# Modulation weights in tiles of four row blocks instead of two

## The chip, the core and the metric

The kernel runs on one NeuronCore of a Trainium2 chip. TensorE (PE) does matrix products, VectorE (DVE), ScalarE (ACT) and GpSimd (POOL) work on elements, and the queue of SyncE (SP) issues nearly all transfers between HBM and the on-chip memory SBUF. TensorE writes its results to PSUM, from where DVE and ACT fetch them. The metric is the device time of one execution in microseconds.

## The reference, cut to what matters

The program is two layers of a diffusion backbone over 1024 latent and 256 context tokens of width 1024. Each layer normalises the tokens, scales and shifts them, projects them by `w_in`, runs four mixers (gated linear attention GLA, neighbourhood attention NA, a diagonal state space model S5, pooling), gates their outputs, projects by `w_out`, normalises and adds. Scale, shift and gate come from a small product, and this is the part that the change touches:

```python
for l in range(DEPTH):   # 2 layers
    shift, scale, gate = jnp.split(jax.nn.silu(c) @ w_mod[l] + b_mod[l], 3, axis=-1)
    shift_c, scale_c, gate_c = jnp.split(jax.nn.silu(c_ctx) @ w_mod[l] + b_mod[l], 3, axis=-1)
    h = rmsnorm(x, g_pre[l]) * (1.0 + scale[:, None]) + shift[:, None]
    ...
    x = x + gate[:, None] * rmsnorm(y @ w_out[l], g_post[l])
```

`w_mod[l]` is 1024 x 3072 in fp32, 12 MB for a layer, and it meets two vectors only: the product is nearly all weight transfer. Everything is fp32.

## The kernel before, in words

The planner that turns the Python into instruction streams keeps one fixed order for each engine. It takes what is ready by its own estimate of times, by priority, and priority is the place in the program unless `later()` adds an amount. So instructions of one helper can be spread between those of others.

`modulation` (line 187) walks over pieces of 512 columns of `w_mod`: two pieces for each of scale, shift and gate. The 1024 rows of a piece are eight blocks of 128 rows. A tile `wm` holds two blocks ([128, 2, 512], 512 KB, 2 KB runs in HBM); a piece takes four tiles. `products` (line 194) takes two tiles, that is four blocks, and gives each block its own group of 32 TensorE columns: block k goes to `state[0][32k:32k+32]`, with `csil`, the silu of the two vectors, as stationary operand. An fp32 matmul is two instructions in the trace, so a call of `products` is eight MATMUL instructions of 512 columns (four from either tile), and a piece is two calls. `rows` copies the PSUM tile to SBUF (line 203). `mod_finish` (line 222) adds the four column groups by another small product and writes either `mcol` (scale and shift) or, for the gate, rows of `dM` in HBM.

`modulation` is a generator: it yields after each load, and whoever holds it calls `next`. `startup` (line 1476) drains that of layer 0's scale and shift, four pieces, before the first normalisation can finish: sixteen loads, tiles in six buffers. The remaining eight pieces run in `run` (line 1532 on): six while layer 0 projects (gate of layer 0, then scale and shift of layer 1) and two while layer 1 does (gate of layer 1). There `self.mods` is advanced by one step after each result of `proj_tok` (line 338) and `proj_cols` (line 323), with three buffers of `wm` and one PSUM bank `pm`. The parameter `lag` (1) and the list `todo` set how far a product stays behind its loads: the first load of a pair is issued with one product still open, the second only after all open products.

Around it in these stages: `s5_proj` and `na_proj` (lines 318 and 334 are the matmuls of all projections), the GLA chunks (lines 934 to 1062), after them S5 and its filler `proj_gates` (line 318 again, evacuated on lines 346 and 347), and the NA phase (lines 1284 to 1460). A branch that all engines pass (line 1555) stands between S5 and NA.

Of the kernel before, what the change touches and what calls it, by code (L numbers as in the profile page):

```python
# [70 lines left out]
class Kernel:  # L71
# [112 lines left out]
        for i in range(2):  # L184
            v.tensor_copy(self.csil[:, :, 32 * i:32 * i + 2], th.rearrange("p (a b) n -> p a b n", b=2)[:, :, i])

    def modulation(self, l, pieces, raws, psum, pool, lag=1):


        nc = self.nc  # L190
        wm = self.a["w_mod"][l].rearrange("(k p) f -> p k f", p=128)
        todo = []

        def products(state, k0, *ws):
            if k0 == 0:
                state.append(psum())
            for k in range(4):
                nc.tensor.matmul(state[0][32 * k:32 * k + 32, :], lhsT=self.csil[:, (k0 + k) // 2, 2 * (k % 2):2 * (k % 2) + 32], rhs=ws[k // 2][:, k % 2, :],
                                 start=(k0 == 0), stop=(k0 == 4))

        def rows(state):
            state.append(self.t([128, 512], "mrow", 2, pool))
            nc.scalar.copy(state[1], state[0])

        for third, q in pieces:
            c0 = third * 1024 + q * 512
            state = []
            for k0 in (0, 4):
                ws = []
                for k in (k0, k0 + 2):  # L210
                    while sum(f.func is products for f in todo) > (lag if k == k0 else 0):
                        todo.pop(0)()
                    ws.append(self.t([128, 2, 512], *next(raws)))
                    nc.sync.dma_start(ws[-1], wm[:, k:k + 2, c0:c0 + 512])
                    yield
                todo.append(partial(products, state, k0, *ws))
            todo += [partial(rows, state), partial(self.mod_finish, l, third, q, state, psum, pool)]
        for f in todo:
            f()
            yield  # L220
# [1255 lines left out]
    def startup(self):  # L1476

        nc, a = self.nc, self.a
        self.silu_c()
        cyc = itertools.cycle  # L1480
        pm = lambda: self.ps2.tile([128, 512], F32, tag="pm", bufs=2, name=self.nm("pm"))
        mods = self.modulation(0, ((1, 0), (0, 0), (1, 1), (0, 1)), cyc([("wm", 6)]), pm, self.mix)
        self.npb = 4
        groups = []
        left = True
        for gi, (t0, n, steps) in enumerate(ORD):
            if not left:
                for g in groups:
                    self.norm_cols(0, *g)
                groups = []  # L1490
            xs = [self.t([128, 1024], "xt", XTB) for _ in range(n)]
            ss = self.t([128, 4], "nss", 3)
            for i, x in enumerate(xs):
                nc.sync.dma_start(x, a["tok"][(t0 + i) * 128:(t0 + i + 1) * 128, :])
                junk = self.t([128, 1024], "stg", 4, self.stg, dtype=mybir.dt.bfloat16)
                if SQ[t0 + i] == "1":
                    nc.vector.tensor_tensor_reduce(junk, x, x, 1.0, 0.0, ALU.mult, ALU.add, ss[:, i:i + 1])
                else:
                    nc.scalar.activation(junk, x, AF.Square, accum_out=ss[:, i:i + 1])
            rs = self.rsqrt(ss[:, :n], [128, n], 1.0 / D, EPS, f"nr{n}")  # L1500
            for i, x in enumerate(xs):
                nc.vector.tensor_scalar(x, x, rs[:, i:i + 1], None, op0=ALU.mult)
            groups.append((t0, xs))
            if gi == WP and WP:
                W = self.load_w(a["w_in"][0][:, 128:416], 288, engines=(cyc([nc.gpsimd]),cyc([nc.vector]), cyc([nc.gpsimd, nc.vector]), cyc([nc.vector,nc.gpsimd]))[SWE])
            for _ in range(steps):
                next(mods, None)
            if steps == 99:
                left = False
            if gi == WP and not WP:  # L1510
                W = self.load_w(a["w_in"][0][:, 128:416], 288, engines=(cyc([nc.gpsimd]),cyc([nc.vector]), cyc([nc.gpsimd, nc.vector]), cyc([nc.vector,nc.gpsimd]))[SWE])
        for g in groups:
            self.norm_cols(0, *g)
        return W

    def run(self):
        nc, a, tc = self.nc, self.a, self.tc
        self.load_consts()
        self.s5p = [None] * DEPTH
        with self.phase("start", True):  # L1520
            with self.phase("x"):
                W = self.startup()
            self.gla_proj(0, False, W)
            self.s5_params(0)
            self.npb = 6
        for l in range(DEPTH):
            last = l == DEPTH - 1
            if last:
                self.gla_proj(l, last)
                with self.phase("par", True):  # L1530
                    self.s5_params(l)
            with self.phase("mods", True) as pool:
                psum = self.ps2
                pm = lambda: psum.tile([128, 512], F32, tag="pm", bufs=1, name=self.nm("pm"))
                todo = ((1, (2,)),) if last else ((0, (2,)), (1, (1, 0)))
                self.npb = 5
                flag = self.gla(l, last)
                self.npb = 6
                raws = itertools.cycle([("wm", 3, pool)])
                mods = itertools.chain(*(self.modulation(i, [(third, q) for third in th for q in range(2)], raws, pm, pool) for i, th in todo))  # L1540
                self.mods = mods
                self.s5_proj(l)
                with self.later():
                    self.na_proj(l, last)
                    for _ in self.mods:
                        pass
            self.npb = 2
            self.s5(l, last)
            self.npb = 6
            ch = CHUNKS[1:] if last else CHUNKS  # L1550
            with self.later():
                self.pool_proj(l, last)
                for m in range(SPLIT[l]):
                    self.proj_gates(l, m, ch)
            with tc.If(nc.values_load(flag, min_val=0, max_val=1) != 0):
                self.gla_general(l, last)
            with self.later(50000, True) as after:
                for m in range(SPLIT[l], 8):
                    self.proj_gates(l, m, ch if m < 8 - RES[l] else ch[:-1])
            self.na(l, last)  # L1560
            tc.cur_priority = after[0]
            with self.phase("out", True):
                self.npb = 2
                for m in range(8 - RES[l], 8):
                    self.proj_gates(l, m, ch[-1:])
                self.out_tiles(l, last)
                self.npb = 6
# [158 lines left out]
```

## Time and profile before

| what | value |
|---|---|
| three runs | 1386.04, 1388.77, 1389.81 us (median 1388.77) |
| profiled execution, its own time | 1390.5 us |
| span of its instructions | 1388.7 us |
| PE busy | 1265.2 us (91%), 6958 matmul instructions |
| PE weight loads | 1011.0 us (73%) |
| DVE / ACT / POOL busy | 66% / 42% / 15% |
| DMA | 231 MB, mean 166 GB/s |
| mean granted TensorE clock | 0.968 |
| matmuls of the modulation (line 198) | 192 instructions |

The profile is of one execution. Times in it count from the first instruction. A matmul's end is modelled, so neighbours overlap in the listing; the distance from one start to the next is what a matmul takes from the stream. The last 1.8 us of the execution's own time lie around the span.

### The profile page before, as it was taken

What the parts mean: (1) busy time and instruction counts of PE and PEld (TensorE: products, weight loads), DVE (VectorE), ACT (ScalarE), POOL (GpSimd) and SP (SyncE); (2) the same over time, 40 slices, a digit from 0 to 9 for tenths busy, and PEclk for the clock granted to TensorE, in tenths of its full rate; (3) what the DMA queues carried; (4) which work ended last, traced back from release to release, by engine and by line L of the source; (5) the groups of instructions that cost most, each with busy time, mean ns of one, the idle gap of its engine ahead of it and who ended that gap; (6) DMA issues with size and microseconds to landing.
All of it is one profiled execution on the core that took longest, in us unless ns stands there. A gap on an engine that the chain in (4) does not pass through costs nothing. (4 is left out here: it accounts for less than half of the span.)

```text
span 1388.7 us, 20066 instructions
## 1 busy us (share of the span) xinstructions
PE 1265.2 (91%) x6958; PEld 1011.0 (73%) x6958; DVE 912.5 (66%) x2269; ACT 584.9 (42%) x1218; POOL 203.8 (15%) x212
## 2 busy tenths in 40 slices
PE   5799999999999999988989999999899998777897
PEld 2698967667777678767878989768667776665676
DVE  2777577456388548773866787586654884776383
ACT  2653443223333347663555644443323333665321
POOL 0100000001100024351410000000112100234220
PEclk9699999999999999999999999999999999998999
DMA  9436685752533267746832475865215535754662
GB/s 330 157 116 224 192 252 166 217 182 76 164 127 113 81 184 197 209 141 208 246 124 92 124 230 188 246 183 157 79 46 185 166 108 161 201 150 139 192 210 91
DMA packets 223477, 231.07 MB, mean 166 GB/s; under 512 B 47016, under 2 KB 176552, under 8 KB 223040
## 3 DMA queue, kind: packets, MB, share of 16 engines
q1 hardware_dynamic: 221776, 227.14, 53.8%
q10 hardware_dynamic: 1584, 2.49, 0.5%
q8 instruction: 58, 0.95, 0.3%
q14 instruction: 59, 0.48, 0.1%
HBM read 159.97 MB, written 69.62 MB: 165 GB/s over the span
## 5 line engine op out<-in xcount | busy, mean ns | idle before, releaser
L318 PE MATMUL pa<-ahi,wh 128*128 128x512 f32 (+1 forms) x664 | 171.7, 387 | 5.0 <-ACT stg L1407 2.1
L318 PE MATMUL pa<-alo,wh 128*128 128x512 f32 (+1 forms) x664 | 166.9, 380 | 0.1
L318 PE MATMUL pa<-ahi,wl 128*128 128x512 f32 (+1 forms) x664 | 165.1, 377 | 0.1
L318 PEld LDWEIGHTS pa<-ahi,wh 128*128 128x128 f32 x664 | 116.0, 193 | 31.8 <-issue 6.4
L318 PEld LDWEIGHTS pa<-alo,wh 128*128 128x128 f32 x664 | 115.7, 192 | 25.7 <-issue 7.9
L318 PEld LDWEIGHTS pa<-ahi,wl 128*128 128x128 f32 x664 | 115.6, 191 | 23.5 <-issue 5.5
L334 PE MATMUL pa<-wh,ahi 128*128 128x256 f32 (+1 forms) x480 | 83.4, 305 | 5.8 <-ACT wh L302 2.4
L303 POOL TENSOR_TENSOR wl<-w,wh 128x1024 fp32r<-128x1024 f32 (+1 forms) x19 | 46.3, 2441 | 286.0 <-PE pa L318 170.8
L388 PE MATMUL po<-wx,ahi 128*128 128x512 f32 x312 | 79.8, 396 | 1.1 <-DVE stg L474 1.0
L334 PE MATMUL pa<-wl,ahi 128*128 128x256 f32 (+1 forms) x480 | 79.6, 299 | 0.1
L1315 PE MATMUL nS<-naK,naQ 128*128 128x256 f32 (+2 forms) x256 | 61.2, 359 | 19.8 <-DVE nast L1322 17.8
L302 ACT CAST wh<-w 128x1024 fp32r<-128x1024 f32 (+1 forms) x51 | 53.8, 1057 | 58.8 <-PE pa L318 36.4
L334 PEld LDWEIGHTS pa<-wh,ahi 128*128 128x128 f32 x480 | 68.8, 197 | 11.4 <-issue 3.3
L334 PE MATMUL pa<-wh,alo 128*128 128x256 f32 (+1 forms) x480 | 76.0, 294 | 0.0
L334 PEld LDWEIGHTS pa<-wl,ahi 128*128 128x128 f32 x480 | 68.1, 195 | 6.6 <-issue 5.3
L1315 PEld LDWEIGHTS nS<-naK,naQ 128*128 128x128 f32 x256 | 46.0, 209 | 32.9 <-DVE nast L1322 28.1
L388 PEld LDWEIGHTS po<-wx,ahi 128*128 128x128 f32 x312 | 59.2, 191 | 14.7 <-DVE stg L474 1.4
L334 PEld LDWEIGHTS pa<-wh,alo 128*128 128x128 f32 x480 | 65.7, 193 | 5.7 <-issue 5.5
L1322 DVE CUSTOM_DVE_ANT_0 naP<-nS,nab 128x640 f32<-128x640 f32 (+1 forms) x64 | 50.3, 787 | 24.3 <-PE nS L1315 12.0
L1327 ACT ACTIVATE naP<-naP,nast 128x640 f32<-128x640 f32 (+1 forms) x64 | 51.5, 805 | 25.1 <-DVE nast L1322 22.3
L1382 PE MATMUL nT<-naPT,naV 128*128 128x256 f32 (+3 forms) x368 | 53.4, 284 | 7.9 <-DVE naPT L1367 5.4
L973 POOL TENSOR_TENSOR qs<-QB,ind 128x512 f32<-128x512 f32 x18 | 19.2, 1066 | 275.4 <-PE pb L1062 159.8
(395 smaller groups left out, 2601.6 us busy)
## 6 DMA issues: line engine op xcount, KB each, us to landing
wm<-in_w_mod_dram SPq DMA_DIRECT2D x48, 512.0 KB
w<-in_w_in_dram SPq DMA_DIRECT2D x41, 512.0 KB
s5R<-dR SPq DMA_DIRECT2D x16, 960.0 KB
xt<-in_tok_dram SPq DMA_DIRECT2D x20, 512.0 KB
dR<-sp_R SPq DMA_DIRECT2D x16, 512.0 KB
dG<-stg SPq DMA_DIRECT2D x32, 256.0 KB
w<-in_w_out_dram SPq DMA_DIRECT2D x16, 512.0 KB
naQ<-dQ SPq DMA_DIRECT2D x24, 320.0 KB
```

What stands on the lines that cost most here:

```text
L302: nc.scalar.copy(hi, raw)
L303: (next(engines) if engines else self.eng(2)).tensor_tensor(lo, raw, hi.bitcast(F32), ALU.subtract)
L318: nc.tensor.matmul(ps[:, :t1 - t0], lhsT=w(k), rhs=x[:, k, t0:t1], start=(i == 0), stop=(i == 23))
L334: nc.tensor.matmul(ps[:, :n], lhsT=x[:, k, t * 128:(t + 1) * 128], rhs=w(k), start=(i == 0), stop=(i == 23))
L388: self.nc.tensor.matmul(o, lhsT=x[:, k], rhs=m(k), start=first and i == 0, stop=last and i == len(todo) - 1)
L973: (nc.gpsimd if BD[d] == "p" else nc.vector).tensor_tensor(out, Q.unsqueeze(1).to_broadcast(sh), ind.unsqueeze(2).to_broadcast(sh), ALU.mult)
L1315: nc.tensor.matmul(ps[:, c * 128:(c + n) * 128], lhsT=Qb[:, i, :], rhs=K[:, b * 128:(b + n) * 128], start=(i == 0), stop=(i == 1))
L1322: v.tensor_tensor_reduce(P[:, 0:nk], ps, bias[:, b0:b0 + nk], 1.0, -NEG, ALU.add, ALU.min, nm)
L1327: nc.scalar.activation(P[:, 0:nk], src, AF.Exp, bias=nm, scale=-1.0, accum_out=l1)
L1382: nc.tensor.matmul(out[:, q:q + n], lhsT=w, rhs=x, start=(i == 0), stop=(i == len(todo) - 1))
```

## The change

A tile `wm` now holds four row blocks. In `startup` it is [128, 4, 512] (1 MB, 2 KB runs, three buffers, which is the same memory as six of 512 KB). In the later stages it is [128, 4, 256]: 512 KB as before, but in runs of 1 KB, and a piece of 512 columns is done in two halves of 256. `products` takes one tile and makes the four column groups from it; the four calls (startup: two) of a piece write to the same PSUM tile, each half to its own columns. The loop now issues one load, appends its product, and then runs products until no more than `lag` (1) are open, so a product is emitted one step after its own load. The yields for each piece stay at four in the later stages and fall from four to two in `startup`.

```diff
-        def products(state, k0, *ws):
-            if k0 == 0:
+        def products(state, k0, c0, w):
+            if not state:
                 state.append(psum())
             for k in range(4):
-                nc.tensor.matmul(state[0][32 * k:32 * k + 32, :], lhsT=self.csil[:, (k0 + k) // 2, 2 * (k % 2):2 * (k % 2) + 32], rhs=ws[k // 2][:, k % 2, :],
-                                 start=(k0 == 0), stop=(k0 == 4))
+                nc.tensor.matmul(state[0][32 * k:32 * k + 32, c0:c0 + width], lhsT=self.csil[:, (k0 + k) // 2, 2 * (k % 2):2 * (k % 2) + 32],
+                                 rhs=w[:, k, :], start=(k0 == 0), stop=(k0 == 4), skip_group_check=True)
...
         for third, q in pieces:
-            c0 = third * 1024 + q * 512
+            f0 = third * 1024 + q * 512
             state = []
-            for k0 in (0, 4):
-                ws = []
-                for k in (k0, k0 + 2):
-                    while sum(f.func is products for f in todo) > (lag if k == k0 else 0):
+            for c0 in range(0, 512, width):
+                for k0 in (0, 4):
+                    w = self.t([128, 4, width], *next(raws))
+                    nc.sync.dma_start(w, wm[:, k0:k0 + 4, f0 + c0:f0 + c0 + width])
+                    todo.append(partial(products, state, k0, c0, w))
+                    while sum(f.func is products for f in todo) > lag:
                         todo.pop(0)()
-                    ws.append(self.t([128, 2, 512], *next(raws)))
-                    nc.sync.dma_start(ws[-1], wm[:, k:k + 2, c0:c0 + 512])
                     yield
-                todo.append(partial(products, state, k0, *ws))
...
-        mods = self.modulation(0, ((1, 0), (0, 0), (1, 1), (0, 1)), cyc([("wm", 6)]), pm, self.mix)
+        mods = self.modulation(0, ((1, 0), (0, 0), (1, 1), (0, 1)), cyc([("wm", 3)]), 512, pm, self.mix)
...
-                mods = itertools.chain(*(self.modulation(i, [(third, q) for third in th for q in range(2)], raws, pm, pool) for i, th in todo))
+                mods = itertools.chain(*(self.modulation(i, [(third, q) for third in th for q in range(2)], raws, 256, pm, pool) for i, th in todo))
```

## Rows read from the trace of the kernel before

**Rows 1.** The page, busy time of each engine (share of the span, instructions).
```profile
PE 1265.2 (91%) x6958; PEld 1011.0 (73%) x6958; DVE 912.5 (66%) x2269; ACT 584.9 (42%) x1218; POOL 203.8 (15%) x212
```
**Rows 2.** Stretches: length; busy PE, PEld, DVE, ACT, POOL; clock, DMA share, GB/s.
```profile
188.00:310.00 122.00, 118.92 (x637) 79.53 (x636) 81.12 (x202) 42.41 (x93) 7.73 (x9) 1.00 0.68 200
310.00:483.00 173.00, 164.58 (x913) 126.30 (x912) 110.42 (x254) 59.61 (x133) 18.21 (x14) 0.99 0.35 110
885.00:935.00 50.00, 48.50 (x220) 32.50 (x221) 41.37 (x76) 20.31 (x29) 0.00 (x0) 1.00 0.74 210
935.00:1163.00 228.00, 211.36 (x1070) 162.01 (x1068) 147.55 (x328) 75.69 (x171) 28.02 (x18) 0.99 0.39 124
1177.00:1300.00 123.00, 92.25 (x525) 76.19 (x526) 83.74 (x203) 68.92 (x150) 43.38 (x58) 0.90 0.59 158
```
**Rows 3.** The chain that ended last, from 60 to 1175: start, duration, what.
```profile
1163.19 6.84 PE pa L318 x29
...
1172.41 3.75 DMA naQ<-dQ
```
**Rows 4.** The same stretches view, line 198 alone: PE, PEld, clock, DMA share, GB/s.
```profile
0.00:40.00 40.00, 13.56 (x64) 2.24 (x64) 0.88 0.94 342
188.00:310.00 122.00, 22.97 (x96) 3.28 (x96) 1.00 0.68 200
885.00:935.00 50.00, 7.17 (x32) 1.11 (x32) 1.00 0.74 210
```
**Rows 5.** Timeline of PE, 185 to 305: start, duration, line, tiles, count [idle before].
```profile
192.49 1.05 PE L198 MATMUL pm<-wm,csil 128*32 128x512 f32 x4
...
220.89 1.91 PE L198 MATMUL pm<-wm,csil 128*32 128x512 f32 x12
...
241.08 0.64 PE L334 MATMUL pa<-wl,ahi 128*128 128x256 f32 x4
241.65 1.05 PE L198 MATMUL pm<-wm,csil 128*32 128x512 f32 x4
242.63 0.74 PE L334 MATMUL pa<-wl,ahi 128*128 128x256 f32 x4
243.21 1.12 PE L334 MATMUL pa<-wh,alo 128*128 128x256 f32 x8
244.16 1.12 PE L334 MATMUL pa<-wh,ahi 128*128 128x256 f32 x8
...
262.41 0.59 PE L946 MATMUL pb<-Sft,QF 128*128 128x256 f32 x2
262.93 1.05 PE L198 MATMUL pm<-wm,csil 128*32 128x512 f32 x2
...
277.79 1.07 PE L198 MATMUL pm<-wm,csil 128*32 128x512 f32 x8
278.79 1.10 PE L334 MATMUL pa<-wl,ahi 128*128 128x256 f32 x7
```
**Rows 6.** Timeline of PE, 885 to 935, last group of line 198.
```profile
930.84 1.05 PE L198 MATMUL pm<-wm,csil 128*32 128x512 f32 x4
```
**Rows 7.** Waits of PE, 188 to 310: total us, times, longest.
```profile
PE pm L198 <- DMA wm<-in_w_mod_dram: 0.2, 1, 0.2
```
**Rows 8.** Waits of PE, 880 to 940.
```profile
PE pm L198 <- DMA wm<-in_w_mod_dram: 0.7, 1, 0.7
```
**Rows 9.** Waits of the SP queue, 188 to 310.
```profile
SPq L214 <- PE pm L198: 14.1, 5, 4.2
```
**Rows 10.** Transfers, 8 to 26: packets, bytes and sizes.
```profile
DMA packets 3617, 6.98 MB, mean 388 GB/s; under 512 B 210, under 2 KB 210, under 8 KB 3617
```
**Rows 11.** Transfers, 188 to 310.
```profile
DMA packets 29370, 24.35 MB, mean 200 GB/s; under 512 B 13820, under 2 KB 22012, under 8 KB 29361
```
**Rows 12.** Timeline of the SP queue, 0 to 40.
```profile
4.01 22.93 SPq L214 DMA_DIRECT2D wm<-in_w_mod_dram  x16
```

More of the change, by code (lines that the diff above doesn't have):

```diff
@@ L185, in silu_c, with modulation @@
             v.tensor_copy(self.csil[:, :, 32 * i:32 * i + 2], th.rearrange("p (a b) n -> p a b n", b=2)[:, :, i])
-    def modulation(self, l, pieces, raws, psum, pool, lag=1):
+    def modulation(self, l, pieces, raws, width, psum, pool, lag=1):
         nc = self.nc
```

## The prediction

> **What bounds the kernel now.** I read the busy times first: PE is busy 91% of the span, DVE 66%, everything else less [rows 1]. A mean says little over stages, so the stretches view comes next. In the stretch in which layer 0 does its six pieces (188 to 310 us) PE is busy 118.9 of 122 us at the full clock, in the following one up to the branch 164.6 of 173; in layer 1 it is 48.5 of 50 and then 211.4 of 228 [rows 2]. So PE idles 11.5 us in the 295 us of layer 0 (4%) and 18.1 us in the 278 us of layer 1 (7%). The projections and gates lie at late priority and fill every hole, and that means work taken off PE there brings all behind it forward. The chain of waits supports it: the piece that starts the last stretch is 29 projection matmuls on PE, ended at 1170 us, and only from there does the chain run through transfers and DVE [rows 3], where PE is busy 75% (92.3 of 123 us) [rows 2]. The reader is to see two regimes: PE's own stream sets the time up to 1170 us, and waits set it after. The startup is a third: line 198 has 64 instructions there, PE has holes, and the DMA engines are 94% busy over the first 40 us [rows 4]; the sixteen loads of `wm` alone run at 388 GB/s [rows 10, 12]. There the transfer sets the time.
>
> **What a group of modulation matmuls costs today.** The timeline shows the product of four row blocks mostly torn in two: each half waits for its own tile, so four instructions run, other matmuls follow, and the other four run later. Between 188 and 935 us there are 27 such groups (21 in the first stretch, 6 in the second; the first and the last of them, and the two shapes, are in [rows 5, 6]): 25 single groups of 2 to 8 instructions and two of 12. The price of a single group does not depend on how many column groups it has: the four instructions at 241.65 give way to the next matmul after 0.98 us, the eight at 277.79 after 1.00 us [rows 5]. That is the whole point: half-filled groups are paid like full ones. Around a group there is more. From 241.08 to 243.21 us stand eight projection matmuls and one group in 2.13 us; the same matmuls alone take (244.16 - 243.21) / 8 = 0.119 us each [rows 5]. So a group takes 2.13 - 8 x 0.119 = 1.18 us from the stream, about 0.1 us of it on either side. A group of 12 lasts 1.91 instead of 1.05 us [rows 5], 0.86 us more, which is one more double pass of 512 columns; it costs 2.04 us. The sum before: 25 x 1.18 + 2 x 2.04 = 33.6 us, of it 20 x 1.18 + 2.04 = 25.6 in layer 0 and 8.0 in layer 1. The busy time of line 198 agrees: 22.97 + 7.17 = 30.1 us without the edges [rows 4].
>
> **What it costs after.** Eight pieces give 32 products of 256 columns, eight instructions each, all from one tile, so nothing can tear them by a missing half. The trace has no such group of 256 columns; the nearest row is a full-array fp32 product of 256 columns in front of a modulation group: two instructions, 262.41 to 262.93, 0.52 us [rows 5]. By the other way, a double pass of 512 columns is 0.86 us, of 256 therefore 0.43, and the 0.98 us of a group is 0.86 plus 0.12 for running empty, which gives 0.55. I take 0.55, with 0.2 us at the edges 0.75 us. The sum after: 32 x 0.75 = 24.0 us. PE gains 33.6 - 24.0 = 9.6 us, 7.6 in layer 0 (25.6 - 18.0) and 2.0 in layer 1. The ends: if two products of a piece stand together everywhere, 16 groups cost 1.18 each, 18.9 us, a gain of 14.7; if a group of 256 columns cost as much as one of 512, 32 x 1.18 = 37.8, a loss of 4.2 us.
>
> Each group of the modulation is framed by about 0.3 us in which TensorE runs empty and starts again (1.18 less 0.86) [rows 5]. [...]
>
> **The rest of the change, edit by edit.** Transfers of the later stages: as many, as large, in runs of 1 KB in place of 2 KB. A 2 KB packet takes 18 us x 16 engines / 3407 = 85 ns (3617 packets less 210 small ones) [rows 10]; in the later stretch a packet of 829 bytes in the mean takes 0.68 x 122 x 16 / 29370 = 45 ns [rows 2, 11]. Between the two lies about 51 ns for 1 KB, so a tile needs 32 x 51 = 1.63 us instead of 1.36. That is 24 x 0.27 = 6.5 us of DMA time in a stretch in which the engines are idle 32% of 122 us: off the path, 0 us. The ends are 0 (half of 85 ns) and 1.36 us a tile (85 ns each), which would bring the share from 0.68 to 0.95 and then no longer be hidden. SP: eight issues fewer in the startup, the same number later; its queue already waits 14.1 us for line 198 to free a buffer [rows 9], with the transfers of the projections behind it, and since a group frees its tile by itself as before I take 0. The extra 128 matmul instructions and weight loads stand inside the groups: 0. The copies (`rows`) and `mod_finish` stay as they are: 0.
>
> Startup: the same 8 MB in the same order, in units of 1 MB with 2 MB behind. The last product needs the last byte as before, and it is then one full group, where now a part of it runs ahead of that byte; half a group of 0.98 us either way. The clock can move it too: it is 0.88 in the mean of these 40 us [rows 4], and PE has fewer groups there after; a last group at half speed would be 1 us longer. I take 0, with -1 and +1 as ends.
>
> **The sum.** The gain of 9.6 us reaches the end as far as PE's stream sets it. PE idles 4% and 7% in the two stages for answers from DVE and ACT, and part of the time freed will turn into such waits; I take 0.88, which is 8.4 us. The profiled time of 1390.5 us becomes 1382.1; the median of the runs shown is 1.7 us lower than the profiled one, so 1380.4 us, stated as 1380. With all 14.7 us of the optimistic end and 1 us from startup it is 1373; what comes on top is that the planner's order shifts for everything behind the first changed load, which I can't price and which moves waits of 1 or 2 us each in both directions.
>
> **Rivals.** First, the chain and not PE: the GLA chunks and the S5 steps are chains DVE, PE, ACT that PE's fillers only surround, and with less filler the same waits show as idle PE. For it: DVE is busy 81 of 122 us and 110 of 173 [rows 2]. Against it: only 11.5 us of idle PE in 295 us, and the last link before NA is a filler on PE [rows 3]. Then some 2 us of 9.6 arrive: 1387.
>
> Second, and on the slower side, the load: a product now stands one step behind its own load, where the first tile of a pair had three steps and the second two, in a queue that is emptied in order. PE takes its stream in order too, so a tile that lands late stops the projections behind it. Today 2 of 27 groups are listed as waiting for their tile, 0.2 and 0.7 us [rows 7, 8]. It decides from a mean of 9.6 / 32 = 0.3 us a group; if all 32 wait the 0.7 us of the longest, 22.4 us are lost against 9.6 gained, if half do, 11.2. The latter, with a tail of the projections that come later, gives 1388.8 + 4 = 1393. Against it: the stretch has 32% of free DMA time, and the planner puts a matmul where it believes its tile landed, not right behind the load.
>
> Third, that the change doesn't do what it says: the groups get fuller but not cheaper, because a group's time is mostly fixed. Then 32 x 1.18 = 37.8 against 33.6, 1388.8 + 4 = 1393 at the worst; half of that is no change. Against it stands the 0.52 us row.
>
> **How the numbers follow.** Forecast 0.60 (its own range 1375 to 1385), chain 0.20 (1384 to 1389), load 0.13 (1388 to 1400), fixed price 0.07 (1387 to 1393). The range that holds 8 in 10 takes the first two and half of the others: 1373 to 1392. A measurement of this kernel can't tell less than 0.3% from none, 4.2 us. Faster than 1384.6: nearly all of the forecast and a quarter of the chain case, 0.63; within: the rest of these, a third of the load case and half of the fixed price, 0.23; slower: 0.14.
>
> **What would show it.** Right: line 198 with 320 instructions, 256 of them of 256 columns; its busy time in the two stretches near 32 x 0.62 = 20 us in place of 30.1; groups of eight that give way after 0.55 us; the branch of layer 0 some 7 us earlier and the first part of the NA chain of layer 1 some 8 us earlier. Wrong: groups of eight at 256 columns that take 0.9 us or more, line 198 waiting over 5 us for `wm`, PE's idle time before the branch up by more than 5 us, or a startup that ends over 2 us later.

## The result and the profile after

The changed kernel takes 1375.86 us (median of six runs, 1365.45 to 1380.5) against 1389.29 us of the kernel before in the same session: ratio 0.9891 [0.9865, 0.9917], that is 11 to 19 us less. A second series on another occasion gives 1376.72 against 1390.18, ratio 0.990 [0.9871, 0.993]. The forecast was 1380. The profiled execution of the first series is the lowest of its six (1365.45, 10 us under the median), so its distance of 25 us to the profile before is not the effect. Stages are therefore compared below between three profiles with the old later products and three with the new ones.

The page and line 198 of the changed kernel (stretches: length; busy PE, PEld; clock, DMA share, GB/s); they answer to [rows 1] and [rows 4].

```profile
PE 1244.4 (91%) x7086; PEld 1001.4 (73%) x7086; DVE 909.1 (67%) x2269; ACT 584.0 (43%) x1218; POOL 202.0 (15%) x212
```

```profile
0.00:40.00 40.00, 11.13 (x64) 1.42 (x64) 0.91 0.92 334
184.00:304.00 120.00, 17.98 (x192) 4.63 (x192) 1.00 0.70 204
870.00:921.00 51.00, 4.70 (x64) 1.46 (x64) 1.00 0.76 212
```

These are 320 instructions, 256 of them in the later stages, busy 22.7 us there where 30.1 stood [rows 4]. The DMA share in the stretch of layer 0 is 0.70 after 0.68: the shorter runs of 1 KB cost no visible transfer time.

The timeline of PE in the changed kernel (start, duration, line, tiles, count) answers to [rows 5].

```profile
197.13 0.28 PE L317 MATMUL pa<-ahi,wl 128*128 128x256 f32 x1
197.34 0.64 PE L198 MATMUL pm<-wm,csil 128*32 128x256 f32 x8
197.91 1.10 PE L317 MATMUL pa<-ahi,wl 128*128 128x256 f32 x7
198.84 0.39 PE L317 MATMUL pa<-ahi,wh 128*128 128x512 f32 x1
...
268.97 0.62 PE L198 MATMUL pm<-wm,csil 128*32 128x256 f32 x2
269.52 0.70 PE L945 MATMUL pb<-Sft,QF 128*128 128x256 f32 x2
270.15 0.64 PE L198 MATMUL pm<-wm,csil 128*32 128x256 f32 x8
270.72 1.10 PE L947 MATMUL pb<-vt,at 128*128 128x64 f32 x8
271.66 0.65 PE L949 MATMUL pb<-glSb,QB 128*128 128x256 f32 x2
272.24 0.63 PE L198 MATMUL pm<-wm,csil 128*32 128x256 f32 x6
272.80 0.86 PE L333 MATMUL pa<-wl,ahi 128*128 128x256 f32 x5
```

A full group gives way after 0.57 us (197.34 to 197.91). With its edges it costs 198.84 - 197.13 - 8 x 0.119 = 0.76 us. The lower lines show what was not forecast: a product of eight is torn into two instructions and six, with GLA matmuls between them, and either part takes 0.55 or 0.56 us like a full group. The planner does this to five of the 24 products in layer 0.

Five stretches of both kernels, each between the same two instructions, from the second series: first the kernel before, then after (columns as in [rows 2]). In order: modulation of layer 0 (from a copy of line 1471 near 150 us to the last product), the GLA rest of layer 0 (to the last matmul of line 1062), the NA stage of layer 0 (line 1315 to line 1382), modulation of layer 1 (from the last copy of line 1471), the GLA rest of layer 1.

```profile
150.40:299.50 149.10, 145.24 (x796) 103.55 (x794) 90.84 (x204) 55.71 (x108) 6.96 (x8) 0.99 0.70 206
299.50:351.50 52.00, 48.49 (x272) 38.40 (x273) 29.26 (x95) 16.08 (x41) 6.77 (x6) 1.00 0.30 86
501.20:629.50 128.30, 113.54 (x712) 95.80 (x713) 98.62 (x240) 78.96 (x183) 55.20 (x71) 0.96 0.61 174
870.00:930.40 60.40, 59.38 (x278) 42.46 (x276) 48.25 (x81) 25.91 (x36) 0.00 (x0) 1.00 0.77 221
930.40:1031.70 101.30, 94.09 (x504) 72.71 (x505) 58.88 (x170) 29.81 (x81) 13.04 (x10) 0.98 0.36 104
```

```profile
149.60:296.50 146.90, 143.48 (x899) 106.49 (x897) 89.95 (x203) 55.91 (x108) 6.90 (x8) 0.98 0.73 215
296.50:347.80 51.30, 47.61 (x267) 37.32 (x265) 29.39 (x95) 15.97 (x41) 6.66 (x5) 1.00 0.24 71
496.80:621.10 124.30, 112.33 (x712) 94.62 (x713) 96.63 (x240) 78.96 (x183) 55.56 (x71) 0.96 0.64 180
860.00:922.30 62.30, 58.74 (x311) 43.60 (x309) 48.16 (x81) 25.88 (x36) 0.00 (x0) 0.97 0.76 215
922.30:1018.40 96.10, 91.45 (x500) 70.95 (x500) 55.47 (x170) 29.47 (x81) 13.52 (x10) 1.00 0.38 109
```

The stage that was to gain most gives 2.2 us, the one that was to gain 2 gives none, and two stages in which little or nothing of the change lies, NA of layer 0 and the GLA rest of layer 1, give 4.0 and 5.2. To see why, I split the length of each stretch into three: time in which no matmul runs (idle), time lost to a granted clock below full (an estimate: length of such a piece times the missing share; two matmuls of line 1062 at 1011.48 in before take 1.92 us at a clock of 0.50, such a pair at 997.00 in the repetition of after 1.02 us at 1.00), and the remainder, which is TensorE's work. Means of three profiles each (before, its repetition, startup_only | later_only, after, its repetition); the length as a range, all in us:

| stretch | length | idle | clock | work |
|---|---|---|---|---|
| modulation l0 | 146.5 to 149.7, then 144.7 to 146.9 | 3.4, 3.7 | 1.7, 1.7 | 143.3, 140.3 |
| GLA rest l0 | 52.0 to 53.6, then 51.3 to 52.5 | 3.6, 3.7 | 0.6, 1.1 | 48.3, 47.2 |
| NA l0 | 127.8 to 128.3, then 121.6 to 124.4 | 15.1, 10.6 | 4.8, 4.4 | 108.1, 107.5 |
| modulation l1 | 60.3 to 61.3, then 60.6 to 62.3 | 1.3, 3.5 | 0.0, 1.1 | 59.4, 57.0 |
| GLA rest l1 | 101.4 to 102.6, then 95.6 to 96.1 | 7.9, 4.5 | 1.7, 0.0 | 92.4, 91.3 |
| all after 90 us | 1292.2 to 1298.7, then 1273.6 to 1290.1 | 100.6, 97.6 | 30.3, 30.1 | 1164.1, 1154.4 |

Work falls by 3.0 + 1.1 + 2.4 + 1.1 = 7.6 us in the four stretches that hold the products or their neighbours. Idle time falls by 4.5 in NA of layer 0 and by 3.4 in the GLA rest of layer 1 (with 1.7 of clock), and rises by 2.2 in the modulation of layer 1. The last row sets a limit to this: over everything behind 90 us work falls by 9.7 and idle time by 3.0 only, so a good half of what the two stages save in idle time is lost again elsewhere. The instruction order of the NA stage is the same in both kernels, that of the GLA rest of layer 1 is not.

In the modulation of layer 1 TensorE now waits longer for a reduction on DVE (its waits there: total us, times, longest; repetition of before, then of after). The third line, from the repetition of after, is the piece of the chain that answers [rows 3].

```profile
PE pb L1010 <- DVE glmx L1008: 0.3, 1, 0.3
PE pb L1009 <- DVE glmx L1007: 2.1, 1, 2.1
1150.07 6.84 PE pa L317 x29
```

What happened in NA is seen in the timeline of all engines, first of the kernel before, then after (the repetition of either).

```profile
505.22 2.36 POOL L303 TENSOR_TENSOR wl<-w,wh 128x1024 fp32r<-128x1024 f32 x1 [12.96 <-ACT naP L1327]
505.25 0.16 DVE L1329 RECIPROCAL nast<-nast 128x1 f32<-128x1 f32 x1
...
505.44 2.29 DVE L1330 TENSOR_SCALAR naP<-naP,nast 128x256 f32<-128x256 f32 x1
507.65 0.68 DVE L1322 CUSTOM_DVE_ANT_0 naP<-nS,nab 128x512 f32<-128x512 f32 x1
...
507.88 0.30 PE L1360 MATMUL nT<-c_ident,naP 128*128 128x128 f32 x1 [1.88 <-DVE naP L1330]
```

```profile
500.72 0.35 DVE L1329 TENSOR_SCALAR naP<-naP,nast 128x256 f32<-128x256 f32 x1
500.79 2.56 POOL L302 TENSOR_TENSOR wl<-w,wh 128x1024 fp32r<-128x1024 f32 x1 [13.56 <-ACT naP L1326]
...
501.22 0.41 PE L1359 MATMUL nT<-c_ident,naP 128*128 128x128 f32 x2
```

The same DVE instruction takes 0.35 us when it starts 0.07 us ahead of the weight subtraction on GpSimd, and 2.29 us when it starts 0.22 us behind it: it ends with the GpSimd instruction, and TensorE stands 1.88 us. In the GLA rest of layer 1 it is the kernel before again that pays (its timeline, and two stretches behind it):

```profile
1005.96 2.36 POOL L303 TENSOR_TENSOR wl<-w,wh 128x1024 fp32r<-128x1024 f32 x1 [3.88 <-PE pa L318]
1006.01 2.33 DVE L138 TENSOR_TENSOR grw<-gry 128x4 f32<-128x4 f32 x1
...
1009.31 0.44 PE L960 MATMUL pb<-c_ident,sq 128*128 128x128 f32 x2 [2.36 <-DVE sq L957]
```

```profile
1005.00:1010.00 5.00, 2.64 (x14) 1.92 (x13) 3.89 (x9) 0.86 (x3) 2.36 (x1) 1.00 0.23 65
1010.00:1013.60 3.60, 3.60 (x8) 1.97 (x7) 1.13 (x3) 0.52 (x3) 0.00 (x0) 0.53 0.68 201
```

An operation on 128x4 elements takes 2.33 instead of 0.16 us; there is another at 994.1 (2.35). PE is busy 2.64 of 5 us, and then the granted clock is 0.53 over 3.6 us (1.00 from 1009.5 to 1010.0, 0.50 from 1010.2 to 1013.5). In the new order the DVE chain has passed when GpSimd starts. Over the whole profile before, 31 DVE instructions take both 0.4 us and half more than the median of their kind (the same line, operation, tiles and shape). That is 36.3 us of excess in all, and each of the 31 ends within 0.6 us of the end of a GpSimd instruction; in after it is 27 of 27, with 31.0 us. In the repetitions the excess is 41.1 and 32.1 us.

### The profile page after: what moved, and what is told of

Same layout as the page of the kernel before. It is cut to its first block, busy times and chain, and to the rows that moved or that the text cites. A ratio compares the mean times of both kernels' runs of the same rounds, so it can differ in the third digit from the quotient of the medians.

```text
span 1363.6 us, 20304 instructions
## 1 busy us (share of the span) xinstructions
PE 1244.4 (91%) x7086; PEld 1001.4 (73%) x7086; DVE 909.1 (67%) x2269; ACT 584.0 (43%) x1218; POOL 202.0 (15%) x212
## 5 line engine op out<-in xcount | busy, mean ns | idle before, releaser
L333 PE MATMUL pa<-wh,ahi 128*128 128x256 f32 (+1 forms) x480 | 78.4, 297 | 4.9 <-DVE ahi L260 2.3
L333 PE MATMUL pa<-wl,ahi 128*128 128x256 f32 (+1 forms) x480 | 78.2, 296 | 0.1
L333 PEld LDWEIGHTS pa<-wh,ahi 128*128 128x128 f32 x480 | 65.6, 191 | 10.0 <-issue 3.0
L302 DVE TENSOR_TENSOR wl<-w,wh 128x1024 fp32r<-128x1024 f32 (+1 forms) x32 | 39.8, 1248 | 29.6 <-ACT wh L301 20.1
```

Source lines behind the costliest of these rows:

```text
L302: (next(engines) if engines else self.eng(2)).tensor_tensor(lo, raw, hi.bitcast(F32), ALU.subtract)
L333: nc.tensor.matmul(ps[:, :n], lhsT=x[:, k, t * 128:(t + 1) * 128], rhs=w(k), start=(i == 0), stop=(i == 23))
```

## The experiments

**The repetition.** No edit: both kernels again.

> The kernel before, unchanged, profiled a second time. Both theories need to know how much one profiled execution of the same program wanders. If the order of instructions sets the time, the milestones of the first profile come back within 1 to 2 us each (first projection matmul at 36 us, line 198 ending at 299 us, branch of layer 0 at 483 us, last NA score of layer 0 at 611 us, branch of layer 1 at 1159 us, end at 1389 us) and the time is within 0.3% of itself. If the granted clock and the transfers wander, single milestones move by 3 to 7 us with the program unchanged.

> The changed kernel, unchanged, profiled a second time and timed: ratio 0.986 to 0.992. Theory PE stream: of the distance to the kernel before, 6 to 8 us arise between 188 and 300 us and between 885 and 935 us and stay to the end, and stages whose order of instructions is the same in both (NA of layer 0, 500 to 611 us: 6.3 us shorter in the first profile) show no lasting gain. Rival clock: the first 90 us are again about 5 us shorter, because the clock granted to PE between 34 and 70 us is again higher than the 0.50 to 0.83 of the kernel before.

Measured: 1389.83 against 1390.18 (0.9986 [0.9965, 1.0008]) and 1376.72 (0.990 [0.9871, 0.993]). The effect is there again. Near 90 us, where the tenth instruction of line 846 ends, the first profile of after is 5.0 us ahead of the first of before; but so is the repetition of before, unchanged, by 3.2, and the repetition of after comes 0.7 later than that one: this is the wander of one execution, and the rival of the clock falls. The theory of PE's stream misses too: NA of layer 0, in the same order, stays 4.0 us shorter, and the two modulation stages give 2.2 us and nothing instead of 6 to 8.

**Startup alone, later stages alone.** The old `modulation` is kept beside the new one as `modulation2`.

```diff
-  mods = itertools.chain(*(self.modulation(i, [...], raws, 256, pm, pool) for i, th in todo))
+  mods = itertools.chain(*(self.modulation2(i, [...], raws, pm, pool) for i, th in todo))    # startup_only
-  mods = self.modulation(0, (...), cyc([("wm", 3)]), 512, pm, self.mix)
+  mods = self.modulation2(0, (...), cyc([("wm", 6)]), pm, self.mix)                          # later_only
```

> Only the startup uses 1 MB tiles of four row blocks; the later stages run the products as before, two tiles each. The order of instructions behind 90 us is then that of the kernel before. Theory PE stream: 0 to -1 us, ratio 0.999 to 1.001, since the startup is set by its transfers. Rival clock and earlier start of the projections: -4 to -5 us, ratio 0.996 to 0.997, already there at 90 us.

> Only the later stages use tiles of four row blocks with 256 columns; the startup is as before. The order of instructions in the stages behind 110 us is then that of the changed kernel. Theory PE stream: nearly the whole gain, -7 to -13 us, ratio 0.991 to 0.995, with line 198 busy near 20 us in the two stretches. Rival (the startup's clock brings half of it): -7 us or less, 0.995 or above.

Measured: startup_only 1389.5, 0.9989 [0.9968, 1.001]; later_only 1379.41, 0.9908 [0.9876, 0.9941]. The larger tiles of the startup are worth nothing that can be measured; the later stages carry nearly all.

**One layer at a time.** `modulation(...) if l == 0 else modulation2(...)`, and the same with `l == 1`, startup as before. The order of the other layer stays that of the kernel before.

> The new products only in the later stage of layer 0; the startup and the stage of layer 1 as before. Theory A (a good half of the gain comes from DVE instructions that are no longer held behind a subtraction of the gates' weights on GpSimd): the stage of the modulation of layer 0 is 3 us shorter, the NA stage of layer 0 about 5 us shorter because the naP scaling near 505 us takes 0.35 us again and not 2.27, and the GLA stage of layer 1 keeps its two instructions of 2.3 us; time near 1381, 8 us below the kernel before. Theory B (the time comes only from TensorE's cheaper groups): 4.5 us of TensorE work go, time near 1385, and the NA stage keeps its 128 us.

> The new products only in the later stage of layer 1. Theory A: the stage of layer 0 and the NA stage of layer 0 stay at the lengths of the kernel before, with the naP scaling of 2.27 us near 505 us; in the GLA stage of layer 1 the two squares that took 2.35 and 2.33 us instead of 0.16 are short again, so that this stage is 4 to 6 us shorter; time near 1384. Theory B: 2.6 us of TensorE work go, time near 1387, and the GLA stage of layer 1 is at most 2 us shorter.

Measured: l0_only 1382.92, 0.996 [0.9938, 0.9982]; l1_only 1386.06, 0.9964 [0.9945, 0.9984]; some 5 us each, so, as far as intervals of 3 us let one say, layer 1 brings as much as layer 0 although it holds 8 of the 32 products. The two stretches NA l0 and GLA rest l1 of l0_only, then of l1_only:

```profile
498.20:623.40 125.20, 113.46 (x712) 95.69 (x713) 97.25 (x240) 79.09 (x183) 55.02 (x71) 0.96 0.62 178
925.60:1028.60 103.00, 95.57 (x506) 73.65 (x505) 59.15 (x170) 29.75 (x81) 13.04 (x10) 0.97 0.35 103
```

```profile
506.60:635.30 128.70, 114.69 (x712) 96.16 (x713) 99.18 (x240) 78.98 (x183) 55.78 (x71) 0.95 0.62 174
937.60:1032.80 95.20, 91.47 (x499) 70.97 (x500) 55.38 (x170) 29.34 (x81) 13.51 (x10) 1.00 0.38 110
```

Each shortening stands only where its layer has the new products. PE's waits in the GLA rest of layer 1 (total us, times, longest) say why. First before (repetition), then l1_only:

```profile
PE pb L960 <- DVE sq L957: 5.7, 7, 2.4
PE pa L318 <- ACT stg L1407: 1.4, 1, 1.4
```

```profile
PE pb L994 <- DVE sq L991: 2.5, 6, 1.5
PE pb L980 <- DVE Sft L1074: 1.0, 1, 1.0
```

l0_only has the first list to the digit (5.7, 7, 2.4), after the second (2.5, 6, 1.5). The naP scaling takes 2.27 us in l1_only (at 510.89) and has no excess in l0_only. Theory A holds on place; in size, l0_only shows 3 us in NA where 5 were expected, and its total is 5.6 by the ratio, with an interval of 2.5 to 8.6 that just holds the 8 expected. The totals alone would hardly decide: theory B's 4 us lie within the interval of l0_only, its 2 us just outside that of l1_only (2.2 to 7.6).

**Shorter GpSimd instructions.** The subtraction of the weights' low part in four instructions. The order on ACT, SP and (but for two instructions of the startup) TensorE stays the same, on DVE some 40 of its 2269 instructions move.

```diff
-  (next(engines) if engines else self.eng(2)).tensor_tensor(lo, raw, hi.bitcast(F32), ALU.subtract)
+  e, s = (next(engines), 2) if engines else (self.eng(2), per)
+  for i in range(0, per, s):
+      e.tensor_tensor(lo[:, i:i + s], raw[:, i:i + s], hi.bitcast(F32)[:, i:i + s], ALU.subtract)
```

> The kernel before, with each subtraction of the gates' low weight part on GpSimd (128x1024, 2.4 us) issued as four of 128x256; the order of all other instructions on each engine stays as it is. Theory A (DVE is held until a whole GpSimd instruction ends): the twelve DVE instructions that this subtraction lengthens, by 22.5 us in all, are held for at most about 0.8 us each, 9 us in all; the NA stage of layer 0 goes from 128 to about 123 us and the GLA stage of layer 1 from 102 to about 97; time near 1379. Theory B (these long instructions are covered by other work): within 2 us of the kernel before, 1389, or a few us slower, since four short ones take about 3.2 us where one takes 2.4.

> The kernel after with the same four-way split. Theory A: its nine DVE instructions behind this subtraction lose 15.7 us in all, three of the twelve of before being gone, so that it gains less from the split: time near 1371, and the distance between the two kernels falls from 13 to about 8 us. Theory B: the distance stays at 13 us, time near 1376 or a few us above.

Measured: before_split4 1380.31, 0.9939 [0.9916, 0.9961]; after_split4 1369.58, 0.9852 [0.9822, 0.9883]. The products are untouched in before_split4, and the gain is some three fifths as large as that of the change (8.5 and 13.9 us by the ratios). Its timeline at the place in NA, and its waits in the GLA rest of layer 1:

```profile
505.24 1.47 POOL L305 TENSOR_TENSOR wl<-w,wh 128x256 fp32r<-128x256 f32 x2 [12.91 <-ACT naP L1329]
...
505.47 0.66 DVE L1332 TENSOR_SCALAR naP<-naP,nast 128x256 f32<-128x256 f32 x1
...
506.28 0.30 PE L1362 MATMUL nT<-c_ident,naP 128*128 128x128 f32 x1 [0.25 <-DVE naP L1332]
```

```profile
PE pb L962 <- DVE sq L959: 4.4, 7, 1.7
PE pa L320 <- ACT stg L1409: 1.4, 1, 1.4
```

The scaling is held to 0.66 us, and TensorE waits 0.25 in place of 1.88. In GLA three DVE steps in a row are now held 0.5 us each, so less is saved there; that stretch is 98.7 us instead of 101.4 to 102.6, with no low clock in it. NA of layer 0 is 126.1 us where theory A said 123. So instructions held behind GpSimd do reach the end. Half confirmed: the distance between the two kernels falls to 10.7 us where theory A said 8, and with intervals of 3 us on either ratio that is not told apart from 13. So the split does not show that it takes away the same time as the change. Nor is the excess of DVE a price: by the split it falls only from 36.3 (41.1 in the repetition) to 31.8 us in the kernel before, and in the kernel after it stays (31.0 and 32.1, then 30.8) while the time falls by some 7 us.

**More and less work in the same groups.** Each later product issued twice, or on half its columns. The latter also adds a DVE instruction for each piece, which sets the other half of the sums to zero.

```diff
+            if width == 256:                       # after_dup: the four matmuls once more
+                for k in range(4):
+                    nc.tensor.matmul(..., rhs=w[:, k, :], start=False, stop=(k0 == 4), ...)
...
-   state[0][32 * k:32 * k + 32, c0:c0 + width], ..., rhs=w[:, k, :]
+   state[0][32 * k:32 * k + 32, c0:c0 + 128], ..., rhs=w[:, k, :128]     # after_half, later stages
```

> The kernel after, with each of the 32 later products issued twice into the same sum (the modulation sums of these stages come out doubled): 32 x 0.43 = 13.8 us more work on TensorE, 10.3 in layer 0 and 3.4 in layer 1, in the same groups. The planner orders what lies around them anew. Theory A (time follows TensorE's work at some nine tenths): time near 1388, 12 us above the kernel after. Theory C (the new order decides as much as the work, through what is held behind GpSimd and how long TensorE idles): 4 us or more away from that, and the difference is found as idle time of TensorE in the NA stage of layer 0 or the GLA stage of layer 1.

> The kernel after, where each later product computes only the first 128 of its 256 columns (the other half of these modulation sums is set to zero): 32 x 0.215 = 6.9 us less work on TensorE, with as many groups; again in a new order of the planner. Theory A: time near 1370, 6 us below the kernel after. Theory C: 4 us or more away from that, by idle time of TensorE and not by its work.

Measured: after_dup 1399.86, 1.0089 [1.0057, 1.012], 23 us above after; after_half 1381.42, 0.993 [0.9905, 0.9956], by the medians 5 us above after although it has less to do (the two intervals overlap; theory A's 1370 lies clearly outside). The split after 90 us, against the mean of the three profiles with the new products (idle 97.6, clock 30.1, work 1154.4): after_dup 99.3, 38.2, 1170.2; after_half 108.9, 31.2, 1149.8. Work moves about as computed (+15.8 for 13.8, -4.6 for -6.9). In after_half 11 us of idle time eat it twice, more than the wander of the idle time among the six profiles of the table (95.2 to 102.5), and its DVE excess behind GpSimd sums up to 45.6 us where after has 31 to 32; that the one causes the other is not shown in this run. So theory A of this experiment, that time follows TensorE's work, falls there, and theory C stands. In after_dup the time is 12 us above theory A's 1388, as theory C's number had it, but not by its cause: idle time rises by 1.7 us, NA of layer 0 and the GLA rest of layer 1 are as short as in after (123.7 and 95.2 us), and of the rest 8 us are low clock, where single executions of the other kernels with the old or new products show 25.3 to 37.9. What this run shows of theory C is thus open.

**The gate's multiplication off GpSimd.** On top of after_split4, line 377 in two halves, or on DVE.

```diff
-        self.eng(4).tensor_tensor(y, y, g, ALU.mult)
+        for i in range(0, n, 2):                                          # after_split_yt
+            self.eng(4).tensor_tensor(y[:, i:i + 2], y[:, i:i + 2], g[:, i:i + 2], ALU.mult)
+        self.nc.vector.tensor_tensor(y, y, g, ALU.mult)                   # after_yt_dve instead
```

> The kernel with the four-way split, and the multiplication by the gate in the out stages (128x512 on GpSimd, 1.3 us) in two halves as well, same order elsewhere. If the DVE instructions held behind it in the out stages (about 9 us of excess in layer 0 and 6 in layer 1) reach the end, these stages shrink by 2 to 4 us in all: 1366. If they are covered, or the halves take longer on GpSimd, which is itself on the chain there: 1370 to 1373.

> The kernel with the four-way split, and the same multiplication on DVE instead of GpSimd: nothing on GpSimd is left in the out stages to hold DVE, but DVE has some 30 more instructions of about 0.7 us, and their order around changes. If the holding costs the end something: 1366 or below. If DVE's own time bounds the last stage: 1372 or above.

Measured: after_split_yt 1374.92, 0.9891 [0.9867, 0.9915]; after_yt_dve 1361.43, 0.9795 [0.9765, 0.9826], the best of all here, some 14 us below after and 29 below before. The halves do not bring the 2 to 4 us: 1374.92 lies above both forecasts and 5 us above after_split4 (the intervals just overlap), though the DVE excess falls from 30.8 to 22.4 us. With the multiplication on DVE the excess is 16.5. NA and out stage of layer 0 together, after_split4 and then after_yt_dve:

```profile
494.60:752.90 258.30, 238.60 (x1274) 197.52 (x1275) 185.38 (x475) 145.76 (x324) 81.59 (x97) 0.97 0.60 175
```

```profile
495.10:739.40 244.30, 233.54 (x1274) 193.48 (x1275) 187.71 (x498) 145.32 (x324) 52.53 (x74) 1.00 0.63 185
```

This stretch is 14 us shorter: 9 us of idle time (19.7 to 10.8) and 6.9 of low clock go, while DVE has only 2.3 us more to do. The two medians are 8 us apart, so some of the 14 is lost again elsewhere. The out stage of layer 1, from its first matmul of line 389 to the end, gains nothing (126.7 and 129.9 us). DVE's own time does not bound it: DVE is busy 77.4 and 78.2 us there. How much of the 14 us is the holding and how much the order, which changed here too, stays open.

## Why the prediction was right, and which step was not

The time (1376 for 1380) and the direction are as forecast; the gain is 13 to 15 us where 8.4 was forecast. The mechanism, fewer and cheaper passes on TensorE, is right and explains about half of the gain, 7 to 8 us. The rest came from a term that the prediction named and did not price, and that it came as a gain was luck. By steps:

- **TensorE's stream sets the time up to 1170 us.** Right in kind: the chain still reaches NA of layer 1 through the last 29 projection matmuls. They stood at 1163.19 [rows 3] and at 1160.85 in the repetition, and begin at 1150.07 in the repetition of after. That is more than the 7.6 us of work: the stream's idle time is not a fixed share, see below. The sign for it came out by halves: NA of layer 0 starts 4 us earlier in the mean of three profiles (500.5, then 496.1), not 7, and NA of layer 1 13 us earlier (1173.3, then 1160.5), not 8.
- **A group costs the same however many column groups it has.** Right, and shown on both sides: 0.98 and 1.00 us for four and eight instructions of 512 columns [rows 5], 0.55, 0.56 and 0.57 us for two, six and eight of 256.
- **What it costs after.** 0.75 us forecast, 0.76 found. That nothing can tear them by a missing half holds to the letter, but they are torn all the same: the planner tears five products of layer 0, which adds 5 x 0.75 = 3.75 us, and merges two times three into groups of 24 that cost about 1.62 us each, which saves 2 x (3 x 0.75 - 1.62) = 1.3. So 33 groups cost 31 x 0.75 + 2 x 1.62 = 26.5 us, not 24.0, and TensorE gains 7.1 us, not 9.6. The split of the stages gives 7.6. At the edges of a group, where the prediction has TensorE run empty, the traces show weight loads that do not run ahead: in all 27 groups of before and all 33 of after the first load of the group and the first one behind it start within 2 ns of their matmul (at 277.79 and 278.79 in before, at 197.34 and 197.91 in after), elsewhere in these stretches 118 ns ahead in the median. How much of the 0.3 us around a group comes from that is not shown.
- **Transfers, SP, startup at nothing.** Right: DMA share 0.70 after 0.68, SP's wait for line 198 in that stretch 11.4 us after 14.1 [rows 9], PE's waits for `wm` 1.1 and 0.8 us in the two stretches of the first profile of after, startup_only no change. The rival of the late load is out.
- **0.88 of the gain reaches the end.** This step failed as a rule: 7 to 8 us of TensorE's work go, and 13 to 15 us come out at the end. In the modulation of layer 1 none of 2.4 us arrives: TensorE now waits 1.8 to 2.1 us for a reduction on DVE (line 1007), where it waited 0.3 before; that is the first rival, in one stage. In the GLA rest of layer 1 the gain is 6 us with 1.1 us of work, and in NA of layer 0 it is 4 to 6 us with the same order. In these two stages the shift of the planner's order and of a few us in time took three DVE instructions out from behind GpSimd (2.2, 2.2 and 1.9 us), and with them, in the GLA rest, a piece of low clock. The prediction named "waits of 1 or 2 us each in both directions" and did not price them. The runs show such waits as part of the missing term, by place (one layer at a time); the split shows that waits of this kind reach the end, not how much of the change's gain they are. Net of what other stages lose, the idle time that the change saves is 3.0 us behind 90 us. after_half shows the other sign, 11 us more idle time with less work.

What stays open: of the 4.5 us of idle time that NA of layer 0 loses, 1.9 are the held scaling; the rest is spread over waits for DVE, GpSimd and DMA that differ between executions. Open too are 2 of the 9.7 us by which the work behind 90 us falls: the four stretches hold 7.6, the rest is spread over the others and no larger than the wander between profiles of one order (5 us).

## What to carry to other kernels

Count a small product with column groups by groups, not by instructions: a part of a group costs a whole one (here 0.98 us for four instructions and 1.00 for eight of 512 columns, 0.55 for two and 0.57 for eight of 256), so hold a group's operands in one load, and look whether the planner tears it all the same. Before forecasting what freed TensorE time is worth, list the DVE instructions that take much longer than the median of their kind and see which GpSimd instruction they end with: here GpSimd instructions of 2.4 us beside chains of DVE instructions of 0.16 to 0.35 us were a cost (TensorE stood 1.88 and 2.36 us) whose place the edit moved by chance. It can be taken away on purpose: here the split of one kind was worth some 8 us in the kernel before and 7 in the kernel after, and moving the other kind to DVE 8 more, though that changed the order too. Try it before you count on it: splitting the other kind gained nothing, and the excess of the DVE instructions did not tell what either was worth.

## What the runs showed of the hardware

Some DVE instructions that start while a GpSimd `TENSOR_TENSOR` runs end with it: 2.35 us in place of 0.16 on 128x4 elements, 2.29 in place of 0.35 on 128x256. With GpSimd pieces of 0.74 us (128x256) the latter takes 0.66 us and ends 0.15 us behind the first piece, while the second runs. In the rows of NA the DVE instruction that starts 0.07 us ahead of the GpSimd one takes 0.35 us, the one that starts 0.22 us behind it 2.29. Starts that are closer do not tell: in the kernel before an operation of line 138 that starts 0.03 us behind takes 2.35 us, a scan of line 772 that starts 0.04 us behind its usual 0.46. Not every DVE instruction is held. In the kernel before, the reciprocal of one column (line 1329, 128x1) keeps its 0.16 us in all 17 places where it starts under a running GpSimd `TENSOR_TENSOR` and ends over 0.2 us ahead of it. The addition of line 347 (128x512), one operand of which is in PSUM, keeps its 0.69 us in all 8 such places. Of the long DVE instructions, 30 of 31 in before and 25 of 27 in after start while a GpSimd instruction runs, the other three within 0.03 us ahead of one, and all end within 0.6 us of the end of one. What sets the held instructions apart from the others is not shown.

Behind a stop of TensorE in the GLA rest of layer 1 (2.36 us, up to 1009.31 in the kernel before) the granted clock fell to 0.50 (0.53 over 1010.0 to 1013.6), which adds an estimated 3.6 x 0.47 = 1.7 us to the stop. Over the whole stretch the clock is 0.98 in before and in its repetition and 0.97 in l0_only, where the longest wait for line 957 (991 in l0_only) is 2.4 us; it is 1.00 in before_split4, l1_only and the repetition of after, where the longest is 1.7, 1.5 and 1.5 us. Behind the first of the two stops in before (2.15 us, up to 997.38) it did not fall (1.00 over 993 to 1009). Other pieces of low clock come and go between executions of one kernel (modulation of layer 1: 1.00 over 870 to 921 in after, 0.97 over 860 to 922.3 in its repetition), so this is seen at one place and not settled as a rule.
